# An fp32 encoder layer on one core: the sums of the weight pairs, four preparations, and some loads and transposes are given other places in their queues

## The chip, the cores and the metric

The kernel runs on one core of a Trainium2 chip. Its time is device time in microseconds, the median of three runs. TensorE does the matrix products (the profile calls it PE, and PEld for its weight loads), VectorE (DVE) and ScalarE (ACT) the elementwise work, GpSimd (POOL) a little of it, and SyncE (SP) issues nearly all transfers. Every engine takes its instructions in the order of its own list, and an instruction that waits holds up all that stand behind it in that list.

## The reference

One encoder layer, with two branches and gates, on 512 and 256 tokens that share all weights:

```python
h = rms_norm(x, pre_w)
qa, ka, va, za, qn, kn, vn, zn, g = split(h @ w_in)        # 1024 -> 6144 columns
oa = diff_attention(qa, ka, va, ...)                       # 4 heads, two maps each; "A"
ya = (oa * silu(za)) @ w_o_diff
on = neighbourhood_attention(qn, kn, vn, na_rpb)           # 8 heads; "B"
yn = (on * silu(zn)) @ w_o_na
gates = sigmoid(g)
merged = gates[:, :, 0] * ya + gates[:, :, 1] * yn
return x + rms_norm(merged @ w_out, post_w)
```

## The kernel before, in words

All data are fp32. A product of two fp32 matrices is done in three matmuls: each operand is split into a high part (rounded, type fp32r, a copy on ScalarE) and a low part (what is left, a subtraction on VectorE). `split_to` does this, and `split` takes its two tiles from rings of three buffers (tags `hi` and `lo`), so that a split can run three products ahead of TensorE.

The stages are these. First the two value projections (`vA`, `vB`), with the norm's scale worked out beside them. Then 20 pairs of 128-column blocks of the weights: eight for queries and keys (A0 to A3, B0 to B3), four for the branches' silu inputs (z0 to z3), eight for the gates (g0 to g7). `pair` computes the two blocks of a pair with seven half-size products instead of eight (p1, p5, p6, p2, p7, p3, and p4, which is held back until the next pair has run its p1). For this `w_blocks` loads four raw blocks a1, a2, b1, b2 from a ring of six buffers (tag `raw`) and forms four sums on VectorE at once: S1 = b1 + b2, S2 = S1 - a1, S3 = a1 - b1 (written over b1), S4 = a2 - S2. The products p5, p6, p7 and p3 use S1, S2, S3 and S4. A product's partial results are copied from PSUM by ScalarE (`so_far`: m1, m5, u2), and later ones are added by VectorE (`add`).

`weave` mixes the steps of the attention heads into the pairs' matmuls. Its list `steps` holds for each head the scores (`scores`, with the softmax on VectorE and ScalarE), `turn` (four transposes on TensorE into a PSUM tile of tag `t`, of which there are two, copied out as `pT` or `bpT`), `pv` (the product with the values) and `out` (transposes of the head's output, copied out as `uf`). A step that isn't due by a written estimate (`LAT`) lets dense work go first. The outputs of head A3 are carried over in `late` and put into the list of B's first pair.

Behind the pairs stands the gating: `u_prep(k)` loads two tiles (`zt`, `ot`), takes silu (ScalarE), multiplies (VectorE), and splits the result into `uh` (ScalarE) and `ul` (VectorE). Tiles k = 0 to 3 come from branch A, 4 to 7 from branch B. 16 products `y` follow (loop `for n, (c, s) in enumerate(order)`); product n needs the split of its block of `wo` (`o_split`) and u[0..3] or u[4..7]: the first with u[4..7] is n = 3. The gates' values are read back from DRAM (`load_gate`, tile `gt`), multiplied (`gate_mults`) and merged (`mf`). Then come seven products with `wout`, for which GpSimd adds pairs of blocks that `rb_tile` loads (`x_sum`, tile `xs`), the second norm and the output.

The order of the lists: TensorE's is the program's (`mm`, `transpose`). On the other engines a scheduler makes the lists when the kernel is built: of what its own estimate of times takes to be ready, it issues what stands first in the program. So an instruction can move ahead of others that stand before it. `keep_in_program_order` forbids this for one instruction: it is put behind the instruction that stands right before it on its engine in the program (pinned, below). It adds no wait. While `strict[0]` is set, all that goes through `vec`, `act` and `pol` is pinned.

In the profile nearly all elementwise work has line L98 and all matmuls L105, so tiles are told apart by name: `A0p5l` is the low part of p5's operand in pair A0, `g7s` a sum of pair g7, `g7x` a PSUM tile of pair g7.

Of the kernel before, what the change touches and what calls it, by code (L numbers as in the profile page):

```python
# [14 lines left out]
ALU = mybir.AluOpType  # L15
# [69 lines left out]
def encoder(ctx, tc, xT, x_p, x_s, wv, wt, wo, wout, pre_w, post_w, subln, biasA, biasB,  # L85
            lams, y_p, y_s):
    nc = tc.nc

    strict = [False]
# [12 lines left out]
    vec, act, pol = Engine(nc.vector), Engine(nc.scalar), Engine(nc.gpsimd)  # L102
# [31 lines left out]


    prew = const.tile([P, KT], F32, name="prew")
    nc.sync.dma_start(prew, pre_w)

    st = ctx.enter_context(ExitStack())
    spool = pool("start", st, side="right", bufs=1)  # L140
# [16 lines left out]
    def load_raw(src, nm):  # L157
        raw = wpool.tile([P, 512], F32, tag="raw", bufs=6, name=nm)
        nc.sync.dma_start(raw, src)
        return raw  # L160

    def split(raw, nm, dst=None, bufs=3):
        hi = (dst or wpool).tile([P, 512], F32R, tag="hi", bufs=bufs, name=nm + "h")
        lo = (dst or wpool).tile([P, 512], F32R, tag="lo", bufs=bufs, name=nm + "l")
        split_to(hi, lo, raw)
        return hi, lo

    def load_w(src, nm, dst=None, bufs=3):
        return split(load_raw(src, nm), nm, dst, bufs)

    def split_to(hi, lo, src):
        act.copy(hi, src)
        vec.tensor_tensor(lo, src, hi.bitcast(F32), ALU.subtract)
# [11 lines left out]
    def sp_dma(*a):  # L185
        tc.keep_in_program_order(nc.sync.dma_start(*a))

    def start_loads(k):
        first = slice(0, NT if k else NT // 2)
        sp_dma(xk[k][:, first], xT[:, k, first])  # L190
        raws[k] = wpool.tile([P, 512], F32, tag="raw", bufs=6, name=f"wv{k}")
        sp_dma(raws[k], wv[k])
        if k == 0:
            sp_dma(xk[k][:, NT // 2:], xT[:, k, NT // 2:])
# [72 lines left out]
    for k in range(KT):  # L267
        w = split(raws[k], f"wv{k}")
# [29 lines left out]
    w = load_w(wv[KT], "wv8")  # L298
# [50 lines left out]
    for n, k in enumerate(ks):  # L349
        n_mms(list(enumerate(vb_ps)), *xp_hl[k], *w, n == 0, n == KT - 1)  # L350
        if n + 1 < KT:
            w = load_w(wv[KT + ks[n + 1]], f"wv{KT + ks[n + 1]}")
# [29 lines left out]
    gd = [dpool.tile([P, NT], F32, name=f"gd{k}") for k in range(2 * KT)]  # L382
# [22 lines left out]

    def w_blocks(ia, ib, nm):

        a1, a2, b1, b2 = [load_raw(wt[n, :, s * 512:(s + 1) * 512], f"{nm}{n}{s}")
                          for n in (ia, ib) for s in range(2)]
        s1, s2, s4 = [wpool.tile([P, 512], F32, tag="sum", name=f"{nm}s{i}") for i in (1, 2, 4)]  # L410
        vec.tensor_tensor(s1, b1, b2, ALU.add)
        vec.tensor_tensor(s2, s1, a1, ALU.subtract)
        vec.tensor_tensor(b1, a1, b1, ALU.subtract)
        vec.tensor_tensor(s4, a2, s2, ALU.subtract)
        return {"A11": a1, "A12": a2, "A22": b2, "S1": s1, "S2": s2, "S3": b1, "S4": s4}

    def product(ps, w, h, first, nm):

        whi, wlo = split(w, nm)
        more = dict(skip_group_check=not first)  # L420
        for k in range(4):
            wh, wl = whi[:, k * P:(k + 1) * P], wlo[:, k * P:(k + 1) * P]
            rh, rl = hblk[h](k)
            mm(ps, wh, rh, start=first and k == 0, stop=False, **more)
            mm(ps, wh, rl, start=False, stop=False, **more)
            mm(ps, wl, rh, start=False, stop=k == 3, **more)
            yield 0.49

    held = []

    def pair(ia, ib, nm, use):

        w = w_blocks(ia, ib, nm)

        def bank(i):
            return dense_tile(f"{nm}x{i}")[:, 0:HN]

        def so_far(t, x):

            m = cpool.tile([P, HN], F32, tag=t, name=f"{nm}{t}")  # L440
            act.copy(m, x)
            return m

        def add(o, x):
            vec.tensor_tensor(o, o, x, ALU.add)


        x1 = bank(1)
        yield from product(x1, w["A11"], "B11", True, nm + "p1")
        m1 = so_far("m1", x1)  # L450
        if held:
            yield from held.pop()()
        x3 = bank(3)
        yield from product(x3, w["S1"], "T1", True, nm + "p5")
        m5 = so_far("m5", x3)
        yield from product(x1, w["S2"], "T2", False, nm + "p6")
        u2 = so_far("u2", x1)
        x2 = bank(2)
        yield from product(x2, w["A12"], "B21", True, nm + "p2")
        add(m1, x2)  # L460
        use(0, 0, m1)
        yield from product(x1, w["S3"], "T3", False, nm + "p7")
        add(m5, x1)
        use(1, 1, m5)
        yield from product(x3, w["S4"], "B22", False, nm + "p3")
        add(u2, x3)
        use(0, 1, u2)

        def tail():
            yield from product(x1, w["A22"], "T4", False, nm + "p4")  # L470
            yield from use(1, 0, x1) or ()
        held.append(tail)
# [317 lines left out]
    late = []  # L790
    for h in range(4):
# [3 lines left out]
        late = outs_  # L795
        steps += ah
    for pr in range(4):
        bp = b_pair(pr)
        if pr < 3:
            bp.insert(2, bias_step("B", pr + 1))  # L800
        bp[2:2] = late
        late = []
        steps += bp

# [34 lines left out]

    def load_gate(c, s):  # L840
        g = gates[c, s] = gpool.tile([P, NT], F32, tag="g", name=f"gt{c}{s}")
        nc.sync.dma_start(g, gd[2 * c + s])

    cs = (0, 4, 1, 5, 2, 6, 3, 7)
    order = [(c, s) for s in range(2) for c in cs[:3]] + [(c, s) for c in cs[3:] for s in range(2)]
# [13 lines left out]
    def u_prep(k):  # L859

        zp = zpool if k % 2 or k > 3 else ztmp
        zt = zp.tile([P, NT], F32, tag="zt", name=f"zt{k}")
        ot = zp.tile([P, NT], F32, tag="ot", name=f"ot{k}")
        nc.sync.dma_start(zt, zd[k])
        nc.sync.dma_start(ot, od[k])
        act.activation(zt, zt, AF.Silu)
        vec.tensor_tensor(zt, zt, ot, ALU.mult)
        act.activation(u[k][0], zt, AF.Copy, scale=0.5)
        vec.scalar_tensor_tensor(u[k][1], zt, 0.5, u[k][0].bitcast(F32), ALU.mult, ALU.subtract)
# [53 lines left out]

    def rb_tile(src, nm, where):
        t = where.tile([P, 512], F32, tag="rb", bufs=4, name=nm)
        nc.sync.dma_start(t, src)
        return t

    def x_right(k, where):
# [7 lines left out]
    A11, A12, A21, A22, S = [], [], [], [], []  # L937

    def gate_mults(n):
        c, s = order[n]  # L940
        g = gates[c, s]
        for i, y in enumerate(y_ps.pop(n)):
            vec.scalar_tensor_tensor(g[:, halves[i]], g[:, halves[i]], 1.0, y, ALU.add, ALU.mult)
        if s:
            mf = zpool.tile([P, NT], F32, tag="zt", name=f"mf{c}")
            vec.tensor_tensor(mf, gates[c, 0], gates[c, 1], ALU.add)
            return c, mf
# [17 lines left out]
    for n, (c, s) in enumerate(order):  # L965
        if n == 12:
            strict[0] = True
        bank = (dense_tile, sc_tile, dense_tile)[n % 3]
        ps = y_ps[n] = [bank(f"y{c}{s}{i}")[:, 0:HN] for i in range(2)]
        whi, wlo = split_o.pop(n)  # L970
        for k in range(4):
            wh, wl = whi[:, k * P:(k + 1) * P], wlo[:, k * P:(k + 1) * P]
            uh, ul = u[4 * s + k]
            for w_, r_, a, z in ((wh, uh, k == 0, False), (wh, ul, False, False),
                                 (wl, uh, False, k == 3)):
                for i in range(2):
                    mm(ps[i], w_, r_[:, halves[i]], start=a, stop=z)
        o_raw(n + 3)
        if n + 1 < len(order):
            o_split(n + 1)  # L980
        if n < 2:
            for k in (4 + 2 * n, 5 + 2 * n):
                u_prep(k)
        merged = gate_mults(n - 1) if n else None
        for i in gates_at.get(n, ()):
            load_gate(*order[i])
        if pending is not None:
            merge_last(pending)
            pending = None
        if merged:  # L990
            merge_first(*merged)
            if merged[0] >= 4:
                pending = merged[0] - 4
                merge_x(pending)
        if 6 <= n < 10:
            x_sum(n - 6)
        if n in (11, 12):
            for t, a in zip(x_right(n - 11, xpool), (A21, A22)):
                a.append(t)
        if n == 13:  # L1000
            A11 += [load_raw(wout[k, 0], f"wx{k}a") for k in range(4)]
        if n == 14:
            x_split(1, 0, A11[0])
            x_split(1, 1, A11[1], (wpool, "sum", 3), (wpool, "sum", 3))
        if n == 15:
            x_split(1, 2, A11[2])
# [18 lines left out]
    x1 = [tp_tile("o1t0"), tp_tile("o1t1"), sc_tile("o1s")]  # L1025
    x3 = [sc_tile("o3s"), dense_tile("o3d0"), dense_tile("o3d1")]
    c, mf = gate_mults(15)
# [106 lines left out]
    x2 = [dense_tile(f"o2d{i}") for i in range(3)]  # L1134
# [68 lines left out]
```

## Time and profile before

| | us |
|---|---|
| median of three runs (601.42 to 604.97) | 602.58 |
| the profiled execution | 600.87 |
| its span, first to last instruction | 598.9 |
| TensorE busy in the span | 584.1 (98%) |
| VectorE busy | 450.6 (75%) |
| ScalarE busy | 341.7 (57%) |
| GpSimd busy | 27.4 (5%) |

The profiled execution's time is 1.97 us over its span, for what lies around the first and the last instruction. Matmuls are pipelined and their ends are modelled, so that a busy share of 98% does not say that all of that time is work; idle time of TensorE, on the other hand, is listed by what ended it.

### The profile page before, as it was taken

What the parts mean: (1) busy time and instruction counts of PE and PEld (TensorE: products, weight loads), DVE (VectorE), ACT (ScalarE), POOL (GpSimd) and SP (SyncE); (2) the same over time, 40 slices, a digit from 0 to 9 for tenths busy, and PEclk for the clock granted to TensorE, in tenths of its full rate; (3) what the DMA queues carried; (4) which work ended last, traced back from release to release, by engine and by line L of the source; (5) the groups of instructions that cost most, each with busy time, mean ns of one, the idle gap of its engine ahead of it and who ended that gap; (6) DMA issues with size and microseconds to landing.
All of it is one profiled execution on the core that took longest, in us unless ns stands there. A gap on an engine that the chain in (4) does not pass through costs nothing.

```text
span 598.9 us, 9826 instructions
## 1 busy us (share of the span) xinstructions
PE 584.1 (98%) x3477; PEld 533.0 (89%) x3477; DVE 450.6 (75%) x954; ACT 341.7 (57%) x776; POOL 27.4 (5%) x31
## 2 busy tenths in 40 slices
PE   9999999999999999999999999999999999999995
PEld 6888899899979889889889989999998999997784
DVE  6769986867695885886775857848766798978687
ACT  8434554675476676576763665756866533325542
POOL 0000000000001001001000000000000041100011
PEclk9999999999999999999999999999999999999999
DMA  8512143232413322332352333223688867435306
GB/s 300 163 39 72 53 153 93 72 120 84 137 49 96 121 89 83 120 119 72 107 166 71 98 132 110 67 80 106 222 274 295 279 197 263 134 106 182 98 17 195
DMA packets 39072, 78.36 MB, mean 131 GB/s; under 512 B 4592, under 2 KB 12144, under 8 KB 38512
## 3 DMA queue, kind: packets, MB, share of 16 engines
q1 hardware_dynamic: 38880, 77.49, 40.1%
q8 instruction: 27, 0.44, 0.3%
q10 hardware_dynamic: 144, 0.26, 0.1%
q14 instruction: 21, 0.17, 0.1%
HBM read 62.00 MB, written 15.73 MB: 130 GB/s over the span
## 4 chain that ended last, share of the span: by engine, by line
PE 70%; DVE 12%; ACT 7%; DMA 6%; issue 4%; POOL 0%; DVEq 0%; SPq 0%; POOLq 0%; ACTq 0%
PE y L105 11%; PE vad L105 4%; PE g0x L105 3%; ACT p L98 3%; PE B2x L105 3%; PE z0x L105 3%; PE z3x L105 2%; PE g4x L105 2%; PE g3x L105 2%; PE A1x L105 2%; PE g2x L105 2%; PE B3x L105 2%; PE o L105 2%; PE g5x L105 2%; PE A0x L105 2%
## 5 line engine op out<-in xcount | busy, mean ns | idle before, releaser
L98 ACT ACTIVATE p<-p,st 128x512 f32<-128x512 f32 (+1 forms) x48 | 30.9, 645 | 20.2 <-DVE st L98 20.1
L98 DVE CUSTOM_DVE_ANT_0 p<-sc,tabA 128x512 f32<-128x512 f32 (+1 forms) x48 | 26.9, 595 | 4.6 <-PE sc L105 3.7
L98 ACT ACTIVATE bp<-bp,bst 128x256 f32<-128x256 f32 x48 | 23.8, 498 | 10.9 <-DVE bst L98 7.6
L105 PE MATMUL o<-vA,pT 128*128 128x128 f32 x160 | 22.0, 276 | 0.6 <-ACT pT L98 0.5
L105 PEld LDWEIGHTS o<-vA,pT 128*128 128x128 f32 x160 | 21.0, 191 | 1.4 <-ACT pT L98 1.2
L98 ACT CAST mhx<-mf 128x384 fp32r<-128x384 f32 (+1 forms) x12 | 7.4, 621 | 24.2 <-DVE mf L98 21.8
L98 DVE CUSTOM_DVE_ANT_0 bp<-bs,tabB 128x256 f32<-128x256 f32 x48 | 17.4, 420 | 5.0 <-PE bs L105 5.0
L98 DVE SCALAR_TENSOR_TENSOR gt<-gt,y 128x384 f32<-128x384 f32 x32 | 16.3, 545 | 3.7 <-DMA gt<-gd 2.3
L98 POOL TENSOR_TENSOR fr<-fr,mhalf 128x4 f32<-128x4 f32 (+1 forms) x8 | 6.8, 854 | 239.1 <-DVE fr L98 239.1
L108 PE MATMUL bpt<-ident,bp 128*128 128x128 f32 x96 | 15.3, 282 | 2.1 <-ACT uf L98 1.0
L98 DVE SCALAR_TENSOR_TENSOR p<-p,cf,p 128x512 f32<-128x512 f32 (+1 forms) x24 | 15.9, 661 | 0.6
L108 PEld LDWEIGHTS bpt<-ident,bp 128*128 128x128 f32 x96 | 10.7, 141 | 5.8 <-ACT bpT L98 1.7
L98 ACT COPY bpT<-bpt 128x512 f32<-128x512 f32 x24 | 13.9, 579 | 2.9 <-PE bpt L108 2.7
L98 POOL TENSOR_TENSOR xs<-wx,wx 128x512 f32<-128x512 f32 x4 | 6.1, 1543 | 203.2 <-DMA wx<-wout 203.2
L98 DVE TENSOR_SCALAR bp<-bp,bli 128x256 f32<-128x256 f32 x48 | 14.8, 350 | 0.6
L105 PE MATMUL ob<-bpT,vB 128*64 128x128 f32 x192 | 13.7, 282 | 0.0
L98 DVE TENSOR_TENSOR zt<-zt,ot 128x768 f32<-128x768 f32 x8 | 7.6, 955 | 7.6 <-ACT zt L98 3.2
L105 PEld LDWEIGHTS ob<-bpT,vB 128*64 128x64 f32 x192 | 10.8, 136 | 2.5 <-issue 2.0
L108 PE MATMUL pt<-ident,p 128*128 128x128 f32 x80 | 12.6, 272 | 0.0
L98 ACT ACTIVATE on<-o,fr 128x128 f32<-128x128 f32 x24 | 7.1, 367 | 9.4 <-DVE fr L98 9.4
L98 ACT COPY pT<-pt 128x512 f32<-128x512 f32 (+1 forms) x24 | 12.2, 508 | 0.0
L98 DVE SCALAR_TENSOR_TENSOR lp<-x,prew,hp 128x768 fp32r<-128x768 f32 (+1 forms) x9 | 8.3, 923 | 4.6 <-ACT hp L98 4.6
(4866 smaller groups left out, 2169.0 us busy)
## 6 DMA issues: line engine op xcount, KB each, us to landing
g<-wt SPq DMA_DIRECT2D x32, 256.0 KB, 3.0
gt<-gd SPq DMA_DIRECT2D x16, 384.0 KB, 5.0
wv<-wv SPq DMA_DIRECT2D x16, 256.0 KB, 4.1
A<-wt SPq DMA_DIRECT2D x16, 256.0 KB, 2.7
z<-wt SPq DMA_DIRECT2D x16, 256.0 KB, 2.9
B<-wt SPq DMA_DIRECT2D x16, 256.0 KB, 2.7
tabB<-biasB SPq DMA_DIRECT2D x4, 1024.0 KB, 4.8
wo<-wo SPq DMA_DIRECT2D x16, 256.0 KB, 4.9
```

The source lines that it names most:

```text
L98: x = getattr(self.e, name)(*a, **k)
L105: return tc.keep_in_program_order(nc.tensor.matmul(*a, **k))
L108: return tc.keep_in_program_order(nc.tensor.transpose(*a))
```

## The change

It has six parts.

1. The four sums of a pair no longer run where the scheduler puts them. Each is pinned: S1 behind the low part of p1's split, S2 behind p5's, S3 behind p6's, S4 behind p2's.
2. For the first pair (A0) the order is p1's split, then all four sums (pinned), then p5's split, all ahead of the pair's first matmul in the program.
3. The outputs of head A3 (`late`) go into B's first list behind its first scores instead of behind its second.
4. `u_prep(4)` to `u_prep(7)` are pinned on ScalarE and VectorE: 4 and 5 behind the split of `wo` for n = 1, 6 and 7 behind that for n = 2. Their loads are not.
5. The loads of the gates (`load_gate`) and of the blocks that GpSimd adds and some others of `wout` (`rb_tile`) are pinned on SyncE.
6. The load of the norm's weights (`prew`) goes behind the first half tile of x, and is pinned.

```diff
     prew = const.tile([P, KT], F32, name="prew")
-    nc.sync.dma_start(prew, pre_w)
...
         sp_dma(xk[k][:, first], xT[:, k, first])
+        if k == 0:
+            sp_dma(prew, pre_w)
         raws[k] = wpool.tile([P, 512], F32, tag="raw", bufs=6, name=f"wv{k}")
...
-        vec.tensor_tensor(s1, b1, b2, ALU.add)
-        vec.tensor_tensor(s2, s1, a1, ALU.subtract)
-        vec.tensor_tensor(b1, a1, b1, ALU.subtract)
-        vec.tensor_tensor(s4, a2, s2, ALU.subtract)
-        return {"A11": a1, "A12": a2, "A22": b2, "S1": s1, "S2": s2, "S3": b1, "S4": s4}
+        def form(o, x, y, op):
+            return lambda: tc.keep_in_program_order(nc.vector.tensor_tensor(o, x, y, op))
+
+        sums = [form(s1, b1, b2, ALU.add), form(s2, s1, a1, ALU.subtract),
+                form(b1, a1, b1, ALU.subtract), form(s4, a2, s2, ALU.subtract)]
+        return {"A11": a1, "A12": a2, "A22": b2, "S1": s1, "S2": s2, "S3": b1, "S4": s4}, sums

-    def product(ps, w, h, first, nm):
-        whi, wlo = split(w, nm)
+    def product(ps, w, h, first, nm, sums=None):
+        whi, wlo = w if isinstance(w, tuple) else split(w, nm)
+        if sums:
+            sums.pop(0)()
...
-        yield from product(x1, w["A11"], "B11", True, nm + "p1")
+        if not begun:
+            begun.append(nm)
+            p1 = split(w["A11"], nm + "p1")
+            while sums:
+                sums.pop(0)()
+            w["A11"], w["S1"] = p1, split(w["S1"], nm + "p5")
+        yield from product(x1, w["A11"], "B11", True, nm + "p1", sums)
...
-        yield from product(x3, w["S1"], "T1", True, nm + "p5")
+        yield from product(x3, w["S1"], "T1", True, nm + "p5", sums)
...
-        yield from product(x1, w["S2"], "T2", False, nm + "p6")
+        yield from product(x1, w["S2"], "T2", False, nm + "p6", sums)
...
-        yield from product(x2, w["A12"], "B21", True, nm + "p2")
+        yield from product(x2, w["A12"], "B21", True, nm + "p2", sums)
...
-        bp[2:2] = late
+        bp[1:1] = late
...
-        nc.sync.dma_start(g, gd[2 * c + s])
+        sp_dma(g, gd[2 * c + s])
...
-        nc.sync.dma_start(t, src)
+        sp_dma(t, src)
...
         if n < 2:
+            strict[0] = True
             for k in (4 + 2 * n, 5 + 2 * n):
                 u_prep(k)
+            strict[0] = False
```

## Rows read from the trace of the kernel before

**Rows 1.** The page's first part: busy time, share of the span, instructions.

```profile
PE 584.1 (98%) x3477; PEld 533.0 (89%) x3477; DVE 450.6 (75%) x954; ACT 341.7 (57%) x776; POOL 27.4 (5%) x31
```

**Rows 2.** TensorE's waits: tile and line, releaser, us in total, times, longest.

```profile
PE g7x L105 <- ACT wo00h L98: 1.5, 1, 1.5
...
PE A2x L105 <- ACT A2u L98: 1.0, 1, 1.0
PE bpt L108 <- ACT uf L98: 1.0, 1, 1.0
PE A0x L105 <- DVE A0p5l L98: 0.8, 1, 0.8
PE bpt L108 <- ACT bpT L98: 0.7, 2, 0.6
PE o L105 <- ACT pT L98: 0.5, 1, 0.5
```

**Rows 3.** VectorE's waits, same columns; of eleven on weight loads, first and last.

```profile
DVE z3s L98 <- DMA z<-wt: 2.6, 1, 2.6
...
DVE A0s L98 <- DMA A<-wt: 0.3, 1, 0.3
```

**Rows 4.** Timeline of VectorE, 297 to 309: start, us, operation, [idle before <-releaser].

```profile
301.69 0.69 DVE L98 TENSOR_TENSOR z3s<-z,z 128x512 f32<-128x512 f32 x1 [2.60 <-DMA z<-wt]
...
304.71 0.42 DVE L98 CUSTOM_DVE_ANT_0 bp<-bs,tabB 128x256 f32<-128x256 f32 x1
...
308.73 0.69 DVE L98 TENSOR_TENSOR z3p1l<-z,z3p1h 128x512 fp32r<-128x512 f32 x1
```

**Rows 5.** Timeline of VectorE, 172 to 180: first and last sum of pair g1.

```profile
173.14 0.68 DVE L98 TENSOR_TENSOR g1s<-g,g 128x512 f32<-128x512 f32 x1
...
177.67 0.69 DVE L98 TENSOR_TENSOR g1s<-g,g1s 128x512 f32<-128x512 f32 x1
```

**Rows 6.** Timeline of VectorE, 76 to 79.

```profile
76.74 0.68 DVE L98 TENSOR_TENSOR A0p5l<-A0s,A0p5h 128x512 fp32r<-128x512 f32 x1
```

**Rows 7.** Timeline of ScalarE, 78 to 80.

```profile
78.58 0.48 ACT L98 COPY A0m<-A0x 128x384 f32<-128x384 f32 x1 [1.22 <-DVE l__674 L98]
```

**Rows 8.** Timeline of ScalarE, 455 to 468.

```profile
460.61 0.85 ACT L98 ACTIVATE zt<-zt 128x768 f32<-128x768 f32 x1 [3.79 <-DMA zt<-zd]
...
465.45 0.61 ACT L98 CAST wo40h<-wo 128x512 fp32r<-128x512 f32 x1
```

**Rows 9.** Timeline of VectorE, 457 to 469.

```profile
461.49 0.96 DVE L98 TENSOR_TENSOR zt<-zt,ot 128x768 f32<-128x768 f32 x1 [2.86 <-DMA zt<-zd]
...
462.96 0.55 DVE L98 TENSOR_TENSOR g7m<-g7m,g7x 128x384 f32<-128x384 f32 x1
...
464.30 1.79 DVE L98 TENSOR_TENSOR wo00l<-wo,wo00h 128x512 fp32r<-128x512 f32 x1
```

**Rows 10.** The chain that ended last, 454 to 468: start, us, what.

```profile
454.97 5.62 DMA zt<-zd
...
465.98 2.12 PE y L105 x12
```

**Rows 11.** Timeline of TensorE, 477 to 479.

```profile
478.50 0.51 PE L105 MATMUL y<-uh,wo01h 128*128 128x384 f32 x2
```

**Rows 12.** Timeline of VectorE, 474 to 479.

```profile
478.07 0.96 DVE L98 SCALAR_TENSOR_TENSOR ul<-zt,uh 128x768 fp32r<-128x768 f32 x1 [0.45 <-ACT uh L98]
```

**Rows 13.** Timeline of GpSimd, 463 to 468.

```profile
463.69 1.84 POOL L98 TENSOR_TENSOR xs<-wx,wx 128x512 f32<-128x512 f32 x1 [184.22 <-DMA wx<-wout]
```

**Rows 14.** Timeline of VectorE, 492 to 501.

```profile
496.07 1.02 DVE L98 SCALAR_TENSOR_TENSOR gt<-gt,y 128x384 f32<-128x384 f32 x2 [2.29 <-DMA gt<-gd]
```

**Rows 15.** Busy time by stretch: length, then each engine's busy us (instructions), clock, DMA.

```profile
500.00:525.00 25.00, 24.98 (x142) 24.66 (x141) 23.64 (x39) 8.52 (x16) 5.49 (x4) 1.00 0.58 179
```

**Rows 16.** Timeline of ScalarE, from the start to 6.

```profile
4.26 0.61 ACT L98 ACTIVATE hp<-x,prew 128x384 fp32r<-128x384 f32 x1 [2.04 <-DMA x<-xT]
```

**Rows 17.** Timeline of SyncE's transfers, from the start to 3.

```profile
1.19 0.42 SPq L186 DMA_DIRECT2D x<-xT  x1
```

More of the change, by code (lines that the diff above doesn't have):

```diff
@@ L427, in product @@
             yield 0.49
-    held = []
+    held, begun = [], []
     def pair(ia, ib, nm, use):
-        w = w_blocks(ia, ib, nm)
+        w, sums = w_blocks(ia, ib, nm)
         def bank(i):
```

## The prediction

> **What bounds the kernel now.** I read the page's busy shares first: TensorE is busy for 584.1 of 598.9 us [rows 1], and the change takes no matmul away and adds none. So the only time to be had is TensorE's idle time, and the next view is the list of what it waited for. Six of its rows sum to 5.5 us [rows 2]. The reader is to see that none of them waits for a transfer: they wait for ScalarE and VectorE, each of which is idle for a quarter of the span or more. So the question for each is what stood in front of the late instruction in its engine's list. That is read from VectorE's own waits and from timelines around each place. The start and the end, where TensorE has no work, are touched only through one load.
>
> **Part 1, sums pinned one by one.** Eleven rows of VectorE's waits are for weight blocks that a sum needs, 2.6 us the longest and 0.3 the shortest [rows 3]. The scheduler put the sums where it expected the blocks to have landed; on the chip the first sum of z3 waits 2.60 us, all four then run, and the softmax of B0 (bp) begins behind them at 304.71 [rows 4]. Three of TensorE's six waits come from this. The transposes of B0 wait for a copy (bpT) that this softmax made late (most of the 0.7); those of a head wait for a copy (pT) behind a softmax that stood behind g2's first sum (0.5); and A2's copy (A2u, 1.0) stands on ScalarE behind exponentials whose inputs VectorE finished late, having run g1's four sums between 173.14 and 178.36 [rows 2, 5]. Pinned, S1 comes behind its own pair's p1 split, for z3 at 308.73, 7.0 us later [rows 4], and each of the other three one product further on. No instruction is added: 80 sums of 0.69 us stay 80 sums. I take 1.0 + 0.6 + 0.5 = 2.1 us for the three waits; bounds are 0 (another instruction is late next) and 2.2.
>
> What the pins cost: S2 now stands between p5's split and p6's. A split takes 0.61 + 0.69 us, with the sum 2.0, and the rings let it start two products before TensorE needs it; 12 matmuls take 2.12 [rows 10], so 4.2 us are there and 2.2 left over. A raw block a1 is released by S3 and a2 by S4, so a pair's last load is issued one sum (0.69) later; z3's had landed 7.0 us ahead of where its first sum will stand. Behind a pinned sum on VectorE stand the next softmax and split; I take 0 for it, since the sums stood in that list before, in bunches. The dearer end is the second rival.
>
> **Part 2, the first pair.** TensorE waits 0.8 us for A0p5l [rows 2], which VectorE reaches at 76.74 [rows 6] behind work that was traced ahead of it; now it is ahead of that work. What is late next: p6 writes over x1, so the copy A0m must be out first, and it starts at 78.58, having waited for l__674 [rows 7], the end of VectorE's backlog. The backlog is the same work in another order, so this copy moves only if l__674 goes ahead of the next split's low part (0.68). So 0.1 to 0.8 us are gained; I take 0.4, the middle, as I cannot see the order.
>
> **Part 3, head A3's output.** Its six transposes fill both PSUM tiles of the transposes just before B0's first `turn`, whose second half waited 1.0 us for the copy uf [rows 2]. One step earlier, ScalarE has time for both copies, and by the written estimates the head's output is due before those scores. Gain 0.9, bounds 0 and 1.0.
>
> **Part 4, u_prep(4) to (7).** At the last product of the last pair TensorE waits 1.5 us [rows 2]. The row names wo00h, but the timelines tell another story. ScalarE stood still for 3.79 us in front of a silu whose tile, issued at 454.97, took 5.62 us to land [rows 8, 10]. VectorE stood still for 2.86 us in front of the product with it, and behind that stood the addition g7m, which began at 462.96 and took 0.55 [rows 9]; it reads the PSUM tile that this last product writes. Pinned behind wo40h and its low part, the silu can no longer stand ahead: ScalarE is free for p4's split from 456.82 on (460.61 less 3.79), and the addition needs only p7, which is done a product earlier. Gain 1.4 of 1.5, bounds 0 and 1.5.
>
> The price is at product n = 3, which needs u[7] and wo01. TensorE gets there at 478.50 and u[7]'s low part is done at 479.03 [rows 11, 12]; a product has 24 matmuls, 4.24 us [rows 10], and u[7] is its last quarter, 481.7. Now TensorE is 1.5 us earlier, 480.2. By durations [rows 8, 9, 12]: wo40h can run when p3's buffers come free (462.2, when TensorE began to wait), so from 462.8 silu 0.85, product 0.96, uh (taken like silu) 0.85, ul 0.96 make 466.4 for the first tile and 2.66 more, 469.1, for the second. Their buffers then take the last two tiles; 5.62 later, 474.7, the same chain for u[7] ends at 478.3. So 1.9 us are left over. I take 0.4 us as cost, bounds 0 and 4.9 (third rival).
>
> **Part 5, loads in program order.** VectorE stood 2.29 us in front of a gate's tile [rows 14], because its load stood on SyncE behind blocks of wout that waited for GpSimd. In program order it goes out before them. TensorE's list has no wait from that, so I take 0. Behind the pinned wout loads on SyncE stand loads for products three further on.
>
> This moves GpSimd's four additions, the first at 463.69 [rows 13], to n = 6 to 9, by 4.24 us a product about 491 to 508. The trace shows what such an addition does to VectorE: wo00l took 1.79 us beside one of 1.84, against 0.68 for the same shape [rows 6, 9, 13]. VectorE is busy for 23.64 of 25 us in about the new place [rows 15]. Four times 1.1 us is 4.4; the wait that goes (2.29) and the idle 1.4 leave a lag of 0.7, under the half product (2 us, an estimate) by which a wo split runs ahead: 0. The Trainium skill, "SBUF — State Buffer", section "Who interferes with whom", says that a VectorE instruction with two SBUF inputs and a GpSimd one that reads SBUF exclude each other, the second blocking for all of the first. The trace agrees in kind (1.79 against 0.68). Full blocking, four times the 1.84 of the trace, is the fourth rival.
>
> **Part 6, prew.** The first activation starts at 4.26, having waited for x [rows 16], which is issued second, at 1.19 [rows 17]. It may start sooner by about the length of an issue, 0.42, but the first weight block's transfer is issued when it was before, and its split comes next. So 0 to 0.4; I take 0.2.
>
> **Sum.** 2.1 + 0.4 + 0.9 + 1.4 + 0.2 = 5.0, less 0.4: 4.6 us. The profiled execution's 600.87 would be 596.3. That run lies 1.7 under the median, which I take as the base: 602.58 - 4.6 = 598.0.
>
> **Rivals.** First, the pins do little: an instruction that is only forbidden to go forward leaves the others free, and another one (a silu, a copy, an exponential) is put where the sum was. Parts 3 and 4 hold by themselves (2.3), all else is nil: 600.3. For it: the lists are made from estimates that were wrong before. Against it: the three waits have the same few sums in front of them.
>
> Second, slower: each sum stands at a fixed place, and where that is between a score and its softmax it delays it by 0.69. The trace has a price: three bunches of four (8.3 us of sums) cost TensorE 2.1, a quarter. 16 pairs woven with heads have 64 sums. If half of them stand ahead of a due softmax, 22 us at a quarter are 5.5 lost, with 2.9 gained in the other parts: 605.2. It decides from 17 such sums on (11.6 us of them). Against it: VectorE is idle for a quarter of the span.
>
> Third, u[7] and wo01 late: if wo40h comes as late as before, done at 466.06 [rows 8], the preparations run one after the other, the second buffer is free at 472.3, its tile lands at 477.9, uh is done at 480.6, and wo01's split behind it at 481.9, where TensorE is at 477.0: 4.9 lost of the 5.0, 602.5.
>
> Fourth, VectorE held by GpSimd: four times 1.84 is 7.4, less 3.7 a lag of 3.7, of which 1.7 are not covered: 599.7.
>
> **How the numbers follow.** Chances: forecast 0.58, first rival 0.13, second 0.10, third 0.14, fourth 0.05. About 0.5% (3.0 us) is what a measurement can tell from no change. The forecast, little less than all of the fourth, and a little of the first count as faster: 0.62; most of the first, and the third, as same: 0.27; the second, and a tail of the third, as slower: 0.11. Low end: the six waits in full (5.5) and 0.4 at the start make 596.7, and the spread of the runs below their median (1.2) makes 595.5; I give 595.0. High end: the third rival and a little of the second, 603.0.
>
> **What would show it.** Right: TensorE's list of waits without A2u, uf, bpT and without g7x; VectorE's without weight loads; each sum behind a low part; silu of u[4] behind wo40h. Part 2 shows in the wait before A0's p6. Wrong: TensorE waiting for wo01 or uh near 477 (third), for bpT or pT in many places (second), for a wo low part near 500 (fourth).

## The result and the profile after

The kernel after takes 594.96 us (median of 4 runs, 593.37 to 595.77), the kernel before beside it 603.03 (4 runs): ratio 0.9862, 95% interval 0.9825 to 0.9898, a gain of 8.1 us. The profiled execution takes 593.37 us, its span is 591.2; against the 598.9 of before the gain there is 7.7. Forecast were 4.6 us and 598.0. The direction was right; the time lies 0.04 us under the low end of the range, 595.0. The repetition (after_again, below) has a ratio of 0.9880, a gain of 7.2 us (5.7 to 8.7). Either way the gain is above the 4.6.

The page's first part and TensorE's list of waits, after (columns as in rows 1 and 2):

```profile
PE 580.5 (98%) x3477; PEld 532.6 (90%) x3477; DVE 451.4 (76%) x954; ACT 343.5 (58%) x776; POOL 28.2 (5%) x31
```

```profile
PE warm_ps L105 <- DVE warm L98: 1.2, 1, 1.2
PE A0x L105 <- ACT A0m L98: 1.0, 1, 1.0
PE vad L105 <- ACT wv0h L98: 0.5, 1, 0.5
PE A2x L105 <- ACT A2u L98: 0.3, 1, 0.3
PE bpt L108 <- ACT buf L98: 0.3, 1, 0.3
PE o3s L105 <- DVE x52l L98: 0.2, 1, 0.2
```

Of the six waits of [rows 2] five are gone and A2u is down from 1.0 to 0.3; A0m and buf are new. All rows of before's list sum to 7.2 us, those of after to 3.5. So the list explains 3.7 of the 7.7. Of the rest 3.6 stand in the busy time: with the same 3477 matmuls it fell from 584.1 to 580.5, while all idle time (span less busy, with gaps too small for the list) fell from 14.8 to 10.7, by 4.1. Busy time that goes away without a matmul less was waiting, too. The Trainium skill, "Perfetto Trace Analysis", section "Identifying the Most-Contended Engine", says that the busy share of matmuls is no good measure of how close a kernel is to what the engine can do, because they are pipelined; the 3.6 us agree.

One wait shows how that comes. TensorE's timeline after, about the wait for A0m (start, us, operation, [idle before <-releaser]):

```profile
77.72 0.33 PE L105 MATMUL A0x<-ly__652,A0p5h 128*128 128x384 f32 x1
77.89 0.34 PE L105 MATMUL A0x<-hy__651,A0p5l 128*128 128x384 f32 x1
79.20 0.45 PE L105 MATMUL A0x<-hy__468,A0p6h 128*128 128x384 f32 x1 [0.97 <-ACT A0m L98]
79.48 0.34 PE L105 MATMUL A0x<-ly__469,A0p6h 128*128 128x384 f32 x1
```

In a running stream a matmul starts 0.17 us after the one before, though a row's duration is 0.33. The list counts from the modelled end (77.89 + 0.34), so it gives 0.97; from start to start the wait costs 1.31 - 0.17 = 1.14 (1.13 unrounded). A wait under 0.16 us doesn't appear at all. Below, "spacing" means this: start to start, less what the same pair of operations takes in the stream.

Laid side by side, matmul by matmul, the two profiled executions drift apart at few places. Below are the us of before, how far the kernel after gains (-) or loses (+) there, measured from the steady stretch ahead of the place to the one behind it, and the part that the place belongs to:

```
to 76       -0.17   start (the kernels' first blocks)
 79         +0.16   part 2: A0p5l's wait goes, A0m's comes
 82 to 164  -0.09   none
165 to 169  -0.63   none (a softmax waits for a transfer, below)
180         -0.65   part 1: A2u
222 to 268  -1.21   part 1: pT twice, and what follows
287 to 299  -1.24   part 3: uf
308 to 388  -1.34   part 1: bpT at 308, 348 and 388
432 to 443  +0.31   part 1: the new wait for buf (0.22), and 0.09 near 443
448         -0.43   part 1: g7p1l
464         -1.70   part 4: g7's last product
500         -0.28   none (a wo low part, wo20l)
559 to 560  -0.44   part 5: x30l
```

So in these two executions part 1 is 3.3 us (forecast 2.1), part 3 1.2 (0.9), part 4 1.7 (1.0 net), part 5 0.4 (0), part 2 a loss of 0.2 (gain of 0.4), the start 0.2 (0.2), and 1.0 is no part's. The wait for wo20l is in this one execution of before and in none of the other 17 profiles of this case.

### The profile page after: what moved, and what is told of

Read it like the earlier page. It is cut to its first block, busy times and chain, and to the rows that moved or that the text cites. A ratio compares the mean times of both kernels' runs of the same rounds, so it can differ in the third digit from the quotient of the medians.

```text
span 591.2 us, 9841 instructions
## 1 busy us (share of the span) xinstructions
PE 580.5 (98%) x3477; PEld 532.6 (90%) x3477; DVE 451.4 (76%) x954; ACT 343.5 (58%) x776; POOL 28.2 (5%) x31
## 4 chain that ended last, share of the span: by engine, by line
PE 92%; DVE 3%; ACT 2%; issue 1%; DMA 1%; POOL 0%; SPq 0%; DVEq 0%; POOLq 0%; ACTq 0%
PE y L105 11%; PE vad L105 4%; PE sc L105 3%; PE o L105 3%; PE A3x L105 3%; PE B0x L105 3%; PE g0x L105 3%; PE B2x L105 3%; PE B3x L105 3%; PE z0x L105 3%; PE o1t L105 3%; PE B1x L105 3%; PE g1x L105 3%; PE z2x L105 3%; PE g4x L105 3%; PE z3x L105 3%
## 5 line engine op out<-in xcount | busy, mean ns | idle before, releaser
L98 POOL TENSOR_TENSOR mtz<-mf,mf 128x384 f32<-128x384 f32 x3 | 3.9, 1301 | 212.9 <-DMA gt<-gd 205.2
L98 DVE TENSOR_TENSOR mlx<-mf,mhx 128x384 fp32r<-128x384 f32 (+1 forms) x12 | 9.8, 817 | 1.3 <-ACT mhx L98 1.2
```

The source lines that it names most:

```text
L98: x = getattr(self.e, name)(*a, **k)
```

## The experiments

Theory of the spacing: the steps of the prediction hold, but a wait is worth its spacing, and waits too small for the list count. Rivals: the gain comes from the order of the loads (part 5); or parts give back at a later wait what they gain. Four kernels of a group ran on one chip, with the kernel before; ratios are to that, with 95% intervals. A gain in us is worked out from the ratio; the plain difference of the two medians can be up to 1.1 us smaller. Where a text says how much slower a kernel is than the changed one across groups, it compares ratios with the 0.988 of the last group.

**One part alone.** Before, with one part's lines of the diff and nothing else:

```diff
 p1_only: +sums.pop(0)()              (in product; w_blocks returns the sums)
 p3_only: -bp[2:2] = late             +bp[1:1] = late
 p4_only: +strict[0] = True           (around u_prep(4) to u_prep(7))
 p5_only: -nc.sync.dma_start(g, ...)  +sp_dma(g, ...)   (rb_tile likewise)
```

> Part 1 alone on the kernel before: the four sums of each pair pinned behind the splits, and nothing else of the change. The prediction's theory (a wait is worth what the list of waits gives as idle time): A2u, bpT and pT, 2.1 us. Theory of the spacing (a wait is worth the extra distance from the start of one matmul to the start of the next, which also holds the overlap of a running stream that was lost, and waits too short for the list count as well): 3.2 us, by the places where the trace of the whole change departs from that of before between 170 and 450 us, without the place near 298 (uf). Rival (the pins only help together with the earlier outputs and the pinned preparations): under 1 us.

> Part 3 alone: head A3's outputs one step earlier, all else as before. The prediction: 0.9 us. Spacing: 1.2 us, all of it between 284 and 300 us, and the wait of bpt for uf is gone. Rival (the place was late because of the sums, so part 3 alone trades the wait for another): 0 to 0.3 us.

> Part 4 alone: the four preparations of the gating pinned behind the splits of wo, the loads as before. The prediction: 1.4 gained, 0.4 given back at u[7] and wo01, 1.0 us. Spacing: 1.6 us, nothing given back. Third rival of the prediction (u[7] and wo01 late): no gain, TensorE waits near 477 us.

> Part 5 alone: the loads of the gates and of wout's blocks in program order on SyncE. The prediction: 0. Rival (the order of the loads is where the part of the gain comes from that the prediction doesn't explain): 0.6 us or more, at wo20l near 500 us and at x30l near 559 us, where the whole change is 0.25 and 0.5 us further ahead than just before.

Measured (before 599.87): part 1 597.96, ratio 0.9951 (0.9929 to 0.9973), 2.9 us; part 3 598.24, 0.9970 (0.9952 to 0.9988), 1.8; part 4 599.25, 0.9983 (0.9968 to 0.9999), 1.0; part 5 598.57, 0.9972 (0.9957 to 0.9987), 1.7. The sum is 7.4, near the 7.2 to 8.1 of the whole. These gains are by ratio, and where an expectation further down calls them, or 3.9 and 7.4, gains by medians, it means these; the differences of the medians themselves are 1.9, 1.6, 0.6 and 1.3, in sum 5.5. So the times alone don't decide between spacing and list for a single part: the interval of part 1 (1.6 to 4.3) holds both. Part 4 comes out at the prediction's net 1.0, but its wait is gone in full; part 5 is not 0.

The trace of part 1 alone shows that a gain can be given back. Its timeline of all engines before g7's last product, and the windows about it (columns as in rows 15):

```profile
458.55 0.84 ACT L98 ACTIVATE zt<-zt 128x768 f32<-128x768 f32 x1 [3.64 <-DMA zt<-zd]
...
459.42 0.96 DVE L98 TENSOR_TENSOR zt<-zt,ot 128x768 f32<-128x768 f32 x1 [3.79 <-ACT zt L98]
...
460.30 0.55 DVE L98 TENSOR_TENSOR g7m<-g7m,g7x 128x384 f32<-128x384 f32 x1
...
460.99 0.41 PE L105 MATMUL g7x<-h__496,g7p4h 128*128 128x384 f32 x1 [2.45 <-DVE g7m L98]
```

```profile
458.00:461.00 3.00, 0.55 (x5) 0.26 (x3) 1.58 (x3) 2.45 (x5) 0.00 (x0) 1.00 0.67 254
461.00:465.00 4.00, 4.00 (x14) 4.00 (x15) 4.00 (x5) 2.67 (x6) 1.81 (x1) 0.57 0.77 244
465.00:470.00 5.00, 5.00 (x31) 5.00 (x30) 2.25 (x4) 2.51 (x5) 0.00 (x0) 1.00 0.86 272
```

This is the chain of part 4 as the prediction read it, tile, silu, product, g7m, and here the list itself names g7m and not wo00h. The wait is 2.45 us (spacing 2.61) where before has 1.5, and behind it the granted clock is 0.57 on the mean of 4 us: ten matmuls start 0.32 apart instead of 0.17, 1.5 us more. That execution lost nearly all it had gained. TensorE starts the last matmul ahead of the wait 3.7 us earlier than in before (458.21 against 461.87), the silu starts only 2.1 us earlier (458.55 against 460.61).

**The kernel before again, and two parts left out.** before_again has no edit, p1_p4 is before with the edits of p1_only and p4_only, and in the changed kernel

```diff
 no_p4: -strict[0] = True             (around u_prep(4) to u_prep(7))
 no_p5: -sp_dma(g, ...)               +nc.sync.dma_start(g, ...)   (rb_tile likewise)
```

> The kernel before once more, unchanged, for a second profiled execution on the chip of the other runs. If the 0.72 us between 164 and 170 us are the change's, they stand here as in the first execution; if they come from one transfer issue that took 1.15 us (od, 161.96) instead of 0.33, they are gone. The same for the first 0.7 us (the four kernels with one part each reach 6 us by 0.7 us earlier, though nothing of them is changed there).

> The changed kernel without part 4: the preparations u[4] to u[7] not pinned. If the parts simply add: slower than the changed kernel by 1.0 us (what part 4 alone gave) to 1.6 us (its spacing in before). If the wait grows by what the others gain (the tile of the silu lands when it lands, and TensorE now comes earlier): it waits till some 2.5 us behind the tile's landing, as in the kernel with part 1 alone (tile 458.53, matmul 460.99), that is 2.5 us or more of waiting there, and 1.3 to 2.8 us in all, the higher end if the granted clock falls behind the wait as it did in that kernel.

> The changed kernel without part 5: the loads of the gates and of wout's blocks not pinned. The prediction: 0 us. If the loads' order is worth something, as part 5 alone says (1.7 us by medians, 0.8 to 2.6): slower than the changed kernel by 0.8 to 1.7 us, by waits at the pair g7, at x30l near 552 us, or both. If part 5's gain alone came only through the wait at g7's last product, which part 4 takes out by itself: 0 to 0.4 us.

> Parts 1 and 4 together on the kernel before. If the parts add: 2.9 + 1.0 = 3.9 us faster than before, by the medians of each alone. If part 1 alone lost at the gating what it had won (its TensorE waited 2.6 us at g7's last product where before waited 1.6, and the clock fell behind it), part 4 now saves that too: 4.9 to 5.5 us.

Measured (before 600.41): before_again 599.87, one time; no_p4 596.34, 0.9925 (0.9893 to 0.9957); no_p5 595.61, 0.9912 (0.9880 to 0.9945); p1_p4 595.96, 0.9908 (0.9874 to 0.9942).

The second execution of before is not the first. The wait near 165 us is not in it, and A0p5l waits 0.36 less, while the 76 us ahead of that are the same within 0.04; but g7's last product has a spacing of 2.14 (1.62) and x30l 1.25 (0.28). The wait near 165, a softmax held by the transfer od, is (0.3 to 1.3 us) in 10 of the 14 profiles of the other kernels run and in neither execution of after: with and without each part, so it goes with the execution and with no part of the change. The 0.6 us of the table above are that. Its explanation by one long issue does not hold for all: in no_p4 the issue took 0.32 us and the softmax still waited 1.20.

no_p4 waits again at g7's last product, 0.99 by the list (spacing 1.15). The 2.5 us that a wait growing with the gains asked for did not come; in the six profiles without part 4 it goes from 0.19 to 2.61 (before 1.62 and 2.14). The ends go with the tile: in p5_only (0.19) the silu starts 2.9 us before TensorE is ready for that product, in p1_only (2.61) 0.2 us after. By ratio it is 2.7 us slower than the changed kernel, give or take 2.4. p1_p4 gained 5.5 us by ratio (4.5 by medians) where the sum is 3.9; its interval (3.5 to 7.6) holds both, so that stays open.

no_p5 is 1.9 us slower than the changed kernel by ratio, give or take 2.4, so its time alone shows nothing; its trace shows the missing term: TensorE waits 1.6 us for x30l. SyncE's issues at the end (start, us of the issue), and then the timeline of all engines, without part 5:

```profile
537.79 0.68 SPq L1141 DMA_DIRECT2D xr<-x_p  x1
538.53 1.24 SPq L1141 DMA_DIRECT2D xr<-x_s  x2
542.83 0.35 SPq L158 DMA_DIRECT2D wx2c<-wout  x1
543.22 0.58 SPq L1141 DMA_DIRECT2D xr<-x_p  x1
544.63 0.34 SPq L158 DMA_DIRECT2D wx3c<-wout  x1
```

```profile
552.60 0.69 DVE L98 TENSOR_TENSOR xs<-wx3c,xs 128x512 f32<-128x512 f32 x1 [2.07 <-DMA wx3c<-wout]
...
553.21 0.68 DVE L98 TENSOR_TENSOR x30l<-xs,x30h 128x512 fp32r<-128x512 f32 x1
...
553.95 0.50 PE L105 MATMUL o3s<-x30l,mhx 128*128 128x512 f32 x1 [1.63 <-DVE x30l L98]
```

and after, SyncE's issues and VectorE's timeline:

```profile
537.35 1.81 SPq L185 DMA_DIRECT2D wx<-wout  x4
539.26 0.68 SPq L1141 DMA_DIRECT2D xr<-x_p  x1
542.46 0.33 SPq L158 DMA_DIRECT2D wx2c<-wout  x1
542.83 0.61 SPq L1141 DMA_DIRECT2D xr<-x_s  x1
544.27 0.34 SPq L158 DMA_DIRECT2D wx3c<-wout  x1
```

```profile
549.67 0.69 DVE L98 TENSOR_TENSOR xs<-wx3c,xs 128x512 f32<-128x512 f32 x1
550.27 0.68 DVE L98 TENSOR_TENSOR x30l<-xs,x30h 128x512 fp32r<-128x512 f32 x1
```

xr is the residual x, which the last steps need. Without part 5 four of its transfers (512 KB each) are issued ahead of wx3c, with it two, since the four pinned blocks wx (256 KB each) now stand on SyncE in front of them; in no_p5 the last of these had landed at 532.3. wx3c is issued within 0.4 us of the same time in both, but its sum starts at 552.60 after a wait for the transfer, against 549.67 without one. The Trainium skill, "DMA: Bandwidth & Descriptors", section "Queues, rings and completion order", says that on each transfer engine what one issuing engine has queued is consumed in the order of the ring. The trace agrees as far as it goes: wx3c lands behind all that was issued ahead of it, 7.9 us after its issue without part 5 and 5.3 with it, so that its sum is 2.9 us later. The bytes ahead since 537 us are the same in both (two xr have taken the place of four wx), so it is not their number: from the landing of the transfer in front of them all (postb) to that of wx3c the same bytes take 11.2 us without part 5 and 8.1 with it. Why is not shown. That the order decides is: x30l has a spacing of 0.28 to 1.79 in all eight profiles of this case in which the blocks are not pinned, and none in the ten in which they are.

**Two parts left out, one piece, one step further.** In the changed kernel, for no_p1 in all pairs but the first:

```diff
 no_p1:  -tc.keep_in_program_order(nc.vector.tensor_tensor(o, x, y, op))
         +vec.tensor_tensor(o, x, y, op)
 no_p2:  -if not begun:               (and what stands under it)
 no_rb:  -sp_dma(t, src)
         +nc.sync.dma_start(t, src)
 better: +w["S2"] = split(w["S2"], nm + "p6")     (behind p5's, ahead of p1)
         +m1, m5 pinned; the high parts of p2 and p7 pinned behind them
```

> The changed kernel with the first pair carried one step further: p6's split also ahead of the first matmul, the copy A0m pinned behind it on ScalarE, and p2's and p7's high parts pinned behind the two copies. If TensorE's wait for A0m is worth its spacing (1.13 us; the list gives 0.97): 0.9 to 1.1 us faster than the changed kernel at 80 us and at the end. Rival (the backlog of VectorE and ScalarE at 76 to 79 us only moves the wait on to p6's low part or to p2): 0 to 0.4 us.

> The changed kernel without part 1: the sums of all pairs but the first run where the scheduler puts them. By the waits of the two executions of the kernel before that part 1 takes out (A2u, pT, bpT, four places, 1.8 to 2.9 us by spacing, and up to 1.1 us at g7p1l where single parts waited), less the two new ones that it brings (0.5 at bpt for buf, 0 to 0.5 at g6u): 1.3 to 3 us slower than the changed kernel. The prediction: 2.1. Rival (the pins do little): under 0.5 us.

> The changed kernel with the gates' loads pinned and the loads of wout's blocks not. If part 5's gain is the order of the last loads (without part 5 three of the residual's transfers, xr, are issued ahead of wx2c and four ahead of wx3c; with it one and two, and wx3c lands in 5.3 us instead of 7.9): TensorE waits 1.2 to 1.8 us for x30l, and the kernel is about as slow as the one without all of part 5. If it comes from the gates: no wait at x30l, the changed kernel's time.

> The changed kernel without part 2: the first pair like all others. The wait for A0p5l comes back (0.4 to 0.8 us by the list, 0.6 to 1.0 by spacing) and the wait for A0m (0.97, spacing 1.13) goes: 0.1 to 0.5 us faster than the changed kernel by that, so that part 2 is worth nothing or less. The prediction: 0.4 us slower without it.

Measured (before 600.22): better 594.20, 0.9906 (0.9874 to 0.9938); no_p1 596.98, 0.9945 (0.9927 to 0.9964); no_rb 594.84, 0.9919 (0.9888 to 0.9951); no_p2 593.32, 0.9888 (0.9860 to 0.9917).

no_p1 is the slowest of all that leave one part out, 3.9 us above the changed kernel by the ratios, give or take 1.8. Of its waits, and then of no_rb's:

```profile
PE A2x L105 <- ACT A2u L98: 1.0, 1, 1.0
...
PE g7x L105 <- DVE g7p1l L98: 0.7, 1, 0.7
PE o L105 <- ACT pT L98: 0.3, 1, 0.3
```

```profile
PE o3s L105 <- DVE x30l L98: 1.3, 1, 1.3
...
PE o1t L105 <- DVE x63l L98: 0.6, 1, 0.6
```

What part 1 had taken out is back, so that the pins do little is ruled out. With the gates' loads pinned and the blocks' not, the wait for x30l is there: part 5's gain at the end is in the blocks of wout, not in the gates.

no_p2 waits at neither place of the first pair. VectorE in no_p2, and then after, about the norm's last tile:

```profile
72.49 0.55 DVE L98 TENSOR_TENSOR l__674<-x,h__673 128x384 fp32r<-128x384 f32 x1
...
73.62 0.68 DVE L98 TENSOR_TENSOR A0p5l<-A0s,A0p5h 128x512 fp32r<-128x512 f32 x1
```

```profile
77.34 0.71 DVE L98 TENSOR_TENSOR A0p2l<-A,A0p2h 128x512 fp32r<-128x512 f32 x1
77.94 0.58 DVE L98 TENSOR_TENSOR l__674<-x,h__673 128x384 fp32r<-128x384 f32 x1
```

Part 1 by itself takes the pair's sums out of the backlog, so that l__674 ends at 73.04 and A0p5l is in time. In the changed kernel the four sums and the low parts of p5, p6 and p2 all run ahead of l__674, which then ends at 78.52, as the prediction feared. ScalarE after, and then in better, about the copy A0m:

```profile
78.14 0.62 ACT L98 CAST A0p7h<-A 128x512 fp32r<-128x512 f32 x1 [0.74 <-PE A0x L105]
78.67 0.85 ACT L98 COPY A0m<-A0x 128x384 f32<-128x384 f32 x2
```

```profile
79.05 0.48 ACT L98 COPY A0m<-A0x 128x384 f32<-128x384 f32 x1 [0.68 <-DVE l__674 L98]
```

After, the copy starts 0.15 us behind the end of l__674, and it also stands behind A0p7h, so two things hold it there. In better it was pinned ahead of A0p7h and still waited for l__674 (0.68 us), and TensorE 0.98 for the copy: its place on its own engine was not all that held it. A miss.

**The whole on one chip with the last parts.** after_again and no_p2_again have no new edit; in the changed kernel

```diff
 no_p3: -bp[1:1] = late               +bp[2:2] = late
 no_p6: -sp_dma(prew, pre_w)          +nc.sync.dma_start(prew, pre_w)   (ahead of all loads, as before)
```

> The changed kernel unchanged, on the same chip as the next three. By its first run: ratio to before 0.986. By the parts alone (2.9 + 1.8 + 1.0 + 1.7 = 7.4 us by medians, part 2 and 6 unknown): 0.988. By the prediction: 0.992. It should wait 1.0 us for A0m at 79 us again, and near nothing at x30l.

> The changed kernel without part 2, once more beside the changed kernel on one chip. If the wait for A0m is worth its spacing and nothing takes its place: 1.1 us faster than the changed kernel. If it is made up for behind: 0.

> The changed kernel without part 3: head A3's outputs behind the second scores of B0 as before. The wait of bpt for uf comes back, 0.97 us by the list, 1.13 to 1.2 by spacing, and with it the 0.2 to 0.36 us just before it that the kernels with part 1 alone and with parts 1 and 4 showed: 1.1 to 1.5 us slower than the changed kernel. The prediction: 0.9. Rival (given back at the waits behind it): under 0.5.

> The changed kernel without part 6: prew's load first, as before. The prediction: 0.2 us slower than the changed kernel (0 to 0.4). If the start depends only on when the first blocks land, which differs by up to 1 us between executions of one kernel: no difference.

Measured (before 601.14): after_again 594.45, 0.9880 (0.9856 to 0.9905); no_p2_again 594.18, 0.9869 (0.9845 to 0.9893); no_p3 596.25, 0.9905 (0.9885 to 0.9925); no_p6 594.28, 0.9874 (0.9852 to 0.9895). Part 3 in company is 1.8 us by medians (1.5 by ratio), and its two places show 1.13 and 0.36 of spacing, as expected. Part 6 is worth nothing that can be seen. no_p2_again has no wait for A0m, but in this execution g6u waited behind a silu. TensorE's longest wait in no_p2_again, and ScalarE there:

```profile
PE g6x L105 <- ACT g6u L98: 1.6, 1, 1.6
```

```profile
438.01 0.84 ACT L98 ACTIVATE zt<-zt 128x768 f32<-128x768 f32 x1 [2.81 <-DMA zt<-zd]
438.76 0.82 ACT L98 ACTIVATE uh<-zt 128x768 fp32r<-128x768 f32 x1
439.49 0.46 ACT L98 COPY g6u<-g6x 128x384 f32<-128x384 f32 x1
```

It is part 4's fault once more, in front of an earlier preparation, which the change doesn't pin. In the first execution of no_p2 the same silu stood there 0.83 us and TensorE did not wait. So leaving part 2 out gains 1.1 us at 79 us in both executions profiled, and in one of them 1.6 were lost near 438; g6u is waited for with part 2 as well (0.2 in no_p3 and in better), so that loss is not shown to go with part 2. By ratio (0.9888 and 0.9869, against 0.9880) neither is told from the changed kernel.

## Why the prediction was right or wrong

**Part 1: mechanism right, size wrong.** The waits for A2u, pT and bpT went when the sums were pinned, and no softmax came late for it. The term 2.1 was mis-sized: 3.3 by the places of the profiled pair, 2.9 alone, 3.9 as the last part (the last two by ratio, with 1.3 and 1.8 either way). The failed step is "I take 1.0 + 0.6 + 0.5 = 2.1 us for the three waits; bounds are 0 (another instruction is late next) and 2.2": an upper bound made from the list of waits is none. A wait is some 0.16 us longer by spacing, and two kinds were left out since the list has them small or not at all: smaller waits for pT and bpT (222, 348 and 388 us), and g7p1l, 0.4 in the profiled execution of before, nothing in before_again, 0.8 to 1.1 in the four other profiles without part 1. The price of the pins, taken as 0, was 0.3: the new wait for buf and a little near 443.

**Part 2: the doubt was right, the value not.** The prediction said that the copy A0m moves only if l__674 goes ahead of the next split's low part: it did not, and TensorE's wait for A0m is 1.0 where that for A0p5l was 0.8. The step that failed is to cost part 2 against the kernel before instead of against part 1, which mends the same wait.

**Part 3** is right in its mechanism: the wait for uf, 1.0 by the list, is gone, and by the places that is worth 1.2 where 0.9 was taken.

**Part 4** is right in its story, and the margin too. After, the last low part of u[7] ends at 473.03 and TensorE comes to it at 475.03: 2.0 us left over, forecast 1.9. So the 0.4 us of price were not due, and the third rival did not come.

```profile
472.07 0.96 DVE L98 SCALAR_TENSOR_TENSOR ul<-zt,uh 128x768 fp32r<-128x768 f32 x1 [0.31 <-ACT uh L98]
...
475.03 0.34 PE L105 MATMUL y<-ul,wo01h 128*128 128x384 f32 x1
```

**Part 5: the step that failed outright** is "TensorE's list has no wait from that, so I take 0". The loads were followed for the gates and for GpSimd's four additions, but `rb_tile` also loads four blocks at the end, and what stands behind those on SyncE, the residual's transfers, was not followed. In the execution that was read x30l had a spacing of only 0.28, under the list; it was 0.8 to 1.8 in the seven other profiles without the pinned blocks. So 0 was near for the execution that was read, by luck, and wrong for the kernel: part 5 alone gained 1.7 us (0.8 to 2.6). Of the additions the fourth rival's row came true without its price. After:

```profile
493.32 1.30 POOL L98 TENSOR_TENSOR xs<-wx,wx 128x512 f32<-128x512 f32 x1 [7.68 <-DMA wx<-wout]
493.58 1.58 DVE L98 TENSOR_TENSOR wo60l<-wo,wo60h 128x512 fp32r<-128x512 f32 x1
...
502.01 1.72 POOL L98 TENSOR_TENSOR xs<-wx,wx 128x512 f32<-128x512 f32 x1 [1.71 <-DMA wx<-wout]
...
502.51 1.77 DVE L98 TENSOR_TENSOR wo61l<-wo,wo61h 128x512 fp32r<-128x512 f32 x1
```

Two splits were stretched (0.68 alone), and TensorE waited for neither.

**Part 6**: 0.2 was taken, nothing was found.

**The sum.** From 4.6 to the 7.7 of the profiled pair 3.1 are missing. By the places part 1 gave 1.2 more than taken, part 4 0.7 (0.4 of it the price that was not due), part 5 0.4, part 3 0.3; part 2 gave 0.6 less, and the start was as forecast, though no_p6 gives no sign that part 6 is what did it. The other 1.0, near 165 us and at wo20l, goes with the execution of before that was read, and is chance. The low end failed with the step named under part 1: "the six waits in full" were taken for the most that could go, while TensorE's waits by spacing were longer, and those of other executions larger still. That the time fell just under that end and not just over it is chance, too: with the ratio of after_again, 0.988, it would be 595.8. The mis-sized terms don't hang on that.

## What to carry to other kernels

Price a wait by the distance from one start to the next, not by the idle time of the list, and never bound a gain by a list of one execution: a wait on a transfer was 0.3 us in one and 1.3 in the next of the same kernel. When a load is moved in a queue, write down what stands behind it to the end of the kernel, since what it gains may be that other transfers now come later. Leave out each part of a change in turn: one that mends what another mends already (part 2) shows only so.

## What the runs showed of the hardware

The granted clock fell behind a wait: in the profile of part 1 alone TensorE stood 2.45 us and started three matmuls near the old spacing. From 461 to 465 us the clock was 0.57 on the mean, that is 1.2 GHz for most of it and 2.4 for the rest, which cost another 1.5 us. In before_again a wait of 1.98 us at the same place left it at 1.00:

```profile
461.00:465.00 4.00, 3.22 (x19) 3.25 (x20) 4.00 (x6) 3.17 (x6) 1.86 (x1) 1.00 0.80 241
```

What decides between the two is not shown. Nothing in the list of waits tells of that; the windows do. And the groups differ: the kernel before had medians of 599.9 to 603.0 us in five of them, 3.1 us against a gain of 7 to 8, so that kernels of different groups can only be compared by their ratios. Whether that is the chip or the time of the run is not shown.
